# Two feed-forward down projections of a decoder layer, from plain row blocks to seven block products

## The chip, the cores and the metric

One core of one Trainium2 chip runs the whole program. The metric is device time in microseconds (us) of that core. Three runs of the kernel before took 2435.83 to 2436.16 us, median 2435.97. One more execution was profiled; all rows below are from it.

## What is computed

A decoder layer over 1024 tokens with a model width of 1024, in float32. The stages in order are: a feed-forward half step, two token mixers (attention) that are merged by gates, a second feed-forward half step, and a gated embedding. The change is in the two feed-forward half steps:

```python
D_MODEL, SEQ, D_FF = 1024, 1024, 2816

def swiglu(u, w_in, w_out):
    a, b = jnp.split(u @ w_in, 2, axis=-1)
    return (jax.nn.silu(a) * b) @ w_out

h = h + 0.5 * swiglu(rms_norm(h, ffn1_norm), ffn1_w_in, ffn1_w_out)
...
h = h + 0.5 * swiglu(rms_norm(h, ffn2_norm), ffn2_w_in, ffn2_w_out)
```

`u @ w_in` is the up projection, `hidden @ w_out` the down projection. The hidden matrix is 1024 tokens by 2816 features, 22 feature blocks of 128.

## The kernel before, in words

**Arithmetic.** Every float32 operand is split into a rounded part HI (fp32r) and a remainder LO, and each product is three matmuls: HI by HI, HI by LO, LO by HI (`mm3`, L181 and on; L179 records each matmul). A split is one cast on ScalarE (ACT) and one subtraction on GpSimd (POOL): L138 and L139 in `load_split`.

**Up projection** (class `Up`, matmuls on L397). The up projection is already done by seven block products (Strassen-Winograd) in place of eight. The two halves of the weights' columns, a and b, and the two halves of the tokens give 2x2 blocks. For each feature block f, seven products of 12 matmuls run in the order 1, 6, 5, 2, 7, 3, 4 (the last f: 1, 6, 2, 5, 7, 3, 4). Products 6 and 7 add up in one bank of PSUM: product 6's bank is read by VectorE (DVE) on L420 into the tile `u2`, and only then may product 7 add to it. After product 4 a chain runs on DVE and ACT (L437, L438, L439, L440), and the finished hidden block, 128 features by 1024 tokens, is stored to DRAM (`hid_d`, one transfer of 512 KB, L441). The pool `upb` holds one buffer each of `u2`, `u3`, `p5` and `c21`, and two of `hidf`, the hidden block.

**Down projection** (class `Down`). Feature blocks go in groups of two (the last group has four). For each group, each of 8 token tiles t and each of two column halves c, one PSUM bank adds up 2 x 3 matmuls (128 by 128 weights, 512 columns) and DVE adds the bank to h at once (L253). While a group computes, the next one's hidden blocks and weight rows are loaded in transfers of 512 KB and split by ACT and POOL. In the last group, each finished token tile goes through `norm_tile`: square and sum on ACT (L216), two small operations on POOL (L197, L198), scaling on DVE (L218), and then, 9.5 us later in the order of TensorE (PE), eight transposes of `un` (L183) into two banks, each evicted by ACT (L207) and DVE (L208). `un` has three buffers. h is loaded from DRAM in eight transfers of 512 KB as soon as the up projection's buffers come free (L587, L1177).

**Order of the work.** PE's order is the order of the code, with the deferred transposes put in by a running count of PE's time (`tick`, `defer`). The instructions of the other engines and of the transfer queue (SP) are ordered ahead of time by a list scheduler, by code order among those that are ready in its own timeline; each engine then runs them strictly in that order. PSUM has eight banks, the pool `dpool` six buffers of split operands, `rawp` three buffers of raw loads, and `upool` four large ones.

```python
for f in self.groups[n]:
    ...
    out.append((load_split([(0, self.hid_d[f].unsqueeze(1))], 1024, homes[0]),
                w_rows(self.wo, f * P, 0, 1024, home=homes[1])))
```

Of the kernel before, what the change touches and what calls it, by code (L numbers as in the profile page):

```python
# [19 lines left out]
P = 128  # L20
S = 1024
# [26 lines left out]
def hybrid_layer_kernel(  # L48
# [242 lines left out]


    A_OF = {1: "a11", 2: "a12", 3: "s4", 4: "a22", 5: "s1", 6: "s2", 7: "s3"}

# [6 lines left out]
    class Left:  # L301
# [40 lines left out]
    class Up:  # L342


        def __init__(self, wi, hid_d):
            self.wi, self.hid_d, self.pools, self.ra, self.w = wi, hid_d, {}, {}, {}

# [36 lines left out]
        def block(self, f, left):  # L384
# [83 lines left out]
    class Down:  # L468


        def __init__(self, hid_d, wo):
            self.hid_d, self.wo, self.more, self.n = hid_d, wo, None, 0
            self.groups = [(f, f + 1) for f in range(0, NF - 4, 2)] + [tuple(range(NF - 4, NF))]

        def home(self):

            pool = dpool if self.n % 10 < 6 else self.more
            self.n += 1
            return pool.tile([P, 2, 1024], F32R, tag="D", name="D")

        def load(self, n):
            out = []
            for f in self.groups[n]:
                if n == len(self.groups) - 2:
                    both = upool.tile([P, 2, 2, 1024], F32R, tag="u", name="D2")
                    homes = both[:, 0], both[:, 1]
                else:
                    homes = self.home(), self.home()
                out.append((load_split([(0, self.hid_d[f].unsqueeze(1))], 1024, homes[0]),
                            w_rows(self.wo, f * P, 0, 1024, home=homes[1])))  # L490
            return out

        def run(self, ready, scale, h, prepare, after):
            for n in range(len(self.groups)):
                cur, last = ready, n + 1 == len(self.groups)
                if last:
                    prepare()
                else:
                    ready = self.load(n + 1)
                for t in down_chunk(h, [c[0] for c in cur], [c[1] for c in cur], scale):  # L500
                    if last:
                        after(t)


    hid_d = dram.tile([NF, P, S], F32, name="hid_d")
    st_u = ExitStack()
    ux = phase(st_u, "ux1", 3, "right")
    st_f = ExitStack()
    up = Up(ffn1_w_in, hid_d)
    up.open(st_f, "1", ("wb", "upa"))  # L510
# [64 lines left out]
    up.open(st_f, "1", ("upb",))  # L575
    down = Down(hid_d, ffn1_w_out)
    ready = []
    up.run(left1, ["s2", "a22", "s3", "s4"], lambda: ready.extend(down.load(0)))
    st_f.close()
    st_u.close()  # L580
    st_h = ExitStack()
    hp = phase(st_h, "h", 1, "right")
    st = ExitStack()
    down.more = phase(st, "dmore1", 4)
    h = hp.tile([P, NT, DM], F32, name="h")
    for t in range(NT):
        nc.sync.dma_start(out=h[:, t, :], in_=x[t * P:(t + 1) * P, :])  # L587
    gm = bcast_row(hp, mix_norm, DM)
    um = []

    def after1(t):
        norm_tile(hp, um, h, t, gm)
        nc.sync.dma_start(out=h_spill[t * P:(t + 1) * P, :], in_=h[:, t, :])

    down.run(ready, 0.5, h, lambda: um.extend(new_u()), after1)
    st.close()
    u = um
# [83 lines left out]
    st.close()  # L681
    st_h.close()
    st = ExitStack()
# [447 lines left out]

    up = Up(ffn2_w_in, hid_d)
    left2 = []
# [31 lines left out]
    up.open(st_f, "2", ("wb", "upa", "upb"))  # L1165
    down = Down(hid_d, ffn2_w_out)
    ready = []
    up.run(left2[0], ["a12", "s1", "s2", "s3", "s4", "a22"], lambda: ready.extend(down.load(0)))
    st_f.close()
    st_u.close()  # L1170
    st_h = ExitStack()
    hp = phase(st_h, "h3", 1, "right")
    st = ExitStack()
    down.more = phase(st, "dmore2", 4)
    h = hp.tile([P, NT, DM], F32, name="h3")
    for t in range(NT):
        nc.sync.dma_start(out=h[:, t, :], in_=h_spill[t * P:(t + 1) * P, :])  # L1177
    gp = bcast_row(hp, ple_norm, DM)
    u3 = []
    down.run(ready, 0.5, h, lambda: u3.extend(new_u()), lambda t: norm_tile(hp, u3, h, t, gp))  # L1180
    st.close()

# [27 lines left out]
    st.close()  # L1210
    st_h.close()
    st_p.close()
# [28 lines left out]
```

## Time and profile before

| what | value |
|---|---|
| median of three runs | 2435.97 us |
| the profiled execution, its own time | 2436.7 us |
| its span, first to last instruction | 2434.9 us |
| PE busy | 2355.5 us (97%) |
| DVE / ACT / POOL busy | 57% / 36% / 41% |
| up projections, about | 58 to 495 us, 1672 to 2096 us |
| down projections, about | 495 to 740 us, 2096 to 2341 us |

The profiled execution's own time lies 0.7 us over the median, and its span 1.8 us under its own time. Matmul durations overlap one another in the profile, so what one matmul costs is read from how many start in a stretch, not from its duration.

### The profile page before, as it was taken

The page shows a single profiled execution, that of the slowest core. Times are in us where ns is not written, and L with a number is a line of the kernel's source. Part 1 is how long each engine was busy: PE and PEld are TensorE (multiplying, and loading weights), DVE is VectorE, ACT ScalarE, POOL GpSimd, SP SyncE. Part 2 cuts the span into 40 slices and gives each one's busy share as a digit, 9 for nine tenths or more (in the row PEclk, how much of TensorE's full clock was granted, in tenths as well). Part 3 has the DMA queues.
Part 4 walks back from the last instruction along what each step waited for, and adds up shares of the span by engine and source line. Part 5 has one row for each costly group of instructions (what it writes and reads, how often), then busy time and mean ns, then how long its engine had stood idle before and what let it go on. Part 6 is the DMA issues. An engine that isn't in the chain of part 4 may idle for free.

```text
span 2434.9 us, 29649 instructions
## 1 busy us (share of the span) xinstructions
PE 2355.5 (97%) x11408; PEld 1965.2 (81%) x11408; DVE 1397.2 (57%) x1814; ACT 869.0 (36%) x1434; POOL 1002.0 (41%) x656
## 2 busy tenths in 40 slices
PE   6899999999999999989998998999999999999999
PEld 5788888888888898777777887887888888888887
DVE  5756666455552224657777778557566655455442
ACT  4433232321223233545656666225223323212131
POOL 7444444453523133432123432556444444545220
PEclk8999999999999999999999999999999999999999
DMA  6222222252425424794453566512222222523222
GB/s 218 76 78 78 79 94 88 87 200 88 136 87 141 108 76 120 213 228 101 99 111 89 143 176 193 182 70 78 87 78 84 90 87 78 216 87 121 69 87 78
DMA packets 246718, 279.91 MB, mean 115 GB/s; under 512 B 11696, under 2 KB 195248, under 8 KB 246576
## 3 DMA queue, kind: packets, MB, share of 16 engines
q1 hardware_dynamic: 222640, 244.46, 31.2%
q0 software_dynamic: 23936, 33.56, 6.7%
q8 instruction: 89, 1.46, 0.2%
q14 instruction: 53, 0.43, 0.1%
HBM read 196.19 MB, written 81.79 MB: 114 GB/s over the span
## 4 chain that ended last, share of the span: by engine, by line
PE 55%; DVE 6%; DMA 3%; ACT 2%; issue 2%; POOL 2%; SPq 0%; ACTq 0%; DVEq 0%; POOLq 0%
PE T L179 31%; PE T L397 17%; PE A L179 4%; PE T L183 3%; DVE D L990 1%; DVE D L991 1%; DMA raw<-in_w_in_dram 1%; DMA k_d<-ev 1%; POOL D L139 1%; DVE pt L208 1%; DVE D L1014 0%; POOL hid L258 0%; DVE mx L1010 0%; ACT D L987 0%; ACT D L1012 0%
## 5 line engine op out<-in xcount | busy, mean ns | idle before, releaser
L397 PE MATMUL T<-u,D 128*128 128x512 f32 x3168 | 734.2, 391 | 4.9 <-DVE u L420 2.6
L397 PEld LDWEIGHTS T<-u,D 128*128 128x128 f32 x3168 | 596.3, 189 | 130.8 <-DVE u L420 2.4
L139 POOL TENSOR_TENSOR D<-raw,D 128x1024 fp32r<-128x1024 f32 (+3 forms) x162 | 370.0, 2304 | 470.0 <-ACT D L138 443.8
L179 PE MATMUL T<-D 128*128 128x512 f32 x2208 | 509.3, 391 | 9.9 <-ACT D L207 5.9
L179 PEld LDWEIGHTS T<-D 128*128 128x128 f32 x2208 | 414.4, 189 | 96.8 <-ACT D L207 6.3
L253 DVE SCALAR_TENSOR_TENSOR h<-T,h 128x512 f32<-128x512 f32 x320 | 220.9, 691 | 226.6 <-PE T L179 224.5
L359 POOL TENSOR_TENSOR D<-ts,D 128x1024 fp32r<-128x1024 f32 x88 | 216.6, 2462 | 314.4 <-ACT D L358 314.3
L138 ACT CAST D<-raw 128x1024 fp32r<-128x1024 f32 (+3 forms) x162 | 157.6, 994 | 384.7 <-PE T L179 206.4
L179 PE MATMUL T<-u,D 128*128 128x512 f32 x1152 | 288.6, 398 | 3.4 <-DVE op L940 2.9
L179 PEld LDWEIGHTS T<-u,D 128*128 128x128 f32 x1152 | 213.3, 191 | 45.2 <-DVE op L940 4.4
L358 ACT CAST D<-ts 128x1024 fp32r<-128x1024 f32 x88 | 92.4, 1051 | 286.7 <-PE T L397 272.8
L179 PE MATMUL T<-D,u 128*128 128x512 f32 (+2 forms) x960 | 194.2, 361 | 0.0
L179 PEld LDWEIGHTS T<-D,u 128*128 128x128 f32 x960 | 166.6, 188 | 22.2
L374 DVE TENSOR_TENSOR ts<-raw 128x512 f32<-128x512 f32 x44 | 35.0, 795 | 202.0 <-POOL D L359 200.4
L208 DVE TENSOR_TENSOR pt<-T,pt 128x512 fp32r<-128x512 f32 (+1 forms) x160 | 100.9, 634 | 70.4 <-ACT pt L207 68.8
L359 POOL TENSOR_TENSOR D<-raw,D 128x1024 fp32r<-128x1024 f32 x44 | 120.4, 2737 | 34.1 <-ACT D L358 34.1
L179 PE MATMUL T<-pt,hv 128*128 128x256 f32 (+1 forms) x640 | 114.0, 301 | 13.9 <-DVE pt L208 12.7
L397 PE MATMUL T<-u,wb 128*128 128x512 f32 x528 | 126.8, 389 | 0.0
L179 PE MATMUL A<-hd 128*128 128x512 f32 (+5 forms) x480 | 114.9, 370 | 2.3 <-DMA hd<-sbk_d 1.6
L440 DVE TENSOR_TENSOR hidf<-u,sg 128x512 f32<-128x512 f32 x44 | 111.5, 2533 | 9.8 <-ACT sg L438 9.4
L207 ACT CAST pt<-T 128x512 fp32r<-128x512 f32 (+1 forms) x160 | 86.7, 544 | 83.8 <-PE T L183 82.1
L397 PEld LDWEIGHTS T<-u,wb 128*128 128x128 f32 x528 | 99.1, 188 | 20.6
(190 smaller groups left out, 2807.2 us busy)
## 6 DMA issues: line engine op xcount, KB each, us to landing
raw<-in_ffn_w_in_dram SPq DMA_DIRECT2D x88, 512.0 KB, 4.0
hid_d<-hidf SPq DMA_DIRECT2D x44, 512.0 KB, 2.6
raw<-hid_d SPq DMA_DIRECT2D x44, 512.0 KB, 3.2
raw<-in_ffn_w_out_dram SPq DMA_DIRECT2D x44, 512.0 KB, 3.5
raw<-in_w_in_dram SPq DMA_DIRECT2D x28, 512.0 KB, 4.4
h_spill<-h SPq DMA_DIRECT2D x16, 512.0 KB, 2.6
gate_d<-gate SPq DMA_DIRECT2D x16, 512.0 KB, 3.2
hd<-sbk_d POOLq DMA_DIRECT2D x32, 256.0 KB, 5.1
```

Source lines behind the costliest of these rows:

```text
L138: nc.scalar.copy(d[:, HI, :n], raw[:, :n])
L139: nc.gpsimd.tensor_sub(d[:, LO, :n], raw[:, :n], d[:, HI, :n].bitcast(F32))
L179: nc.tensor.matmul(ps, lhs, rhs, start=start, stop=stop)
L183: nc.tensor.transpose(ps, src, ident)
L207: nc.scalar.copy(hi, ps)
L208: nc.vector.tensor_sub(lo, ps, hi.bitcast(F32))
L253: nc.vector.scalar_tensor_tensor(hs, ps, scale, hs, op0=ALU.mult, op1=ALU.add)
L358: nc.scalar.copy(d[:, HI], src)
L359: nc.gpsimd.tensor_sub(d[:, LO], src, d[:, HI].bitcast(F32))
L374: nc.vector.tensor_sub(ts[:, 0], b12, b11)
L397: nc.tensor.matmul(ps, b[:, l, k], a[:, r, k], start=start and k == n == 0, stop=k == 3 and n == 2, skip_group_check=True)
L440: nc.vector.tensor_mul(t["hid"][:, 512:], u3, sg)
```

## The change

Both down projections are done by the same seven block products as the up projection. The blocks are: token halves by the two feature blocks of a pair on the left, the two feature blocks by column halves on the right. There are 11 pairs of feature blocks. Seven left operands per pair (a11, a12, a22 and the sums s1 to s4) are formed on DVE at the end of the up projection's odd blocks and stored as seven 256 KB pieces. The down projection runs over 77 steps; a step is one product of one pair, 12 matmuls into four banks. Products 1 and 2 alternate pair by pair, then 5, 7, 6, 3 and 4 run over all pairs, one after another. A product's four banks add up over all 11 pairs before they are evicted. The subtraction of a split moves from POOL to DVE, except for the first two pairs. The sums on the right are kept in `upool`. h is loaded within step 10's code, and token tiles are normalised four at a time, after products 3 and 4.

```diff
     def new_u():
-        return [[upool.tile([P, KT, 512], F32R, tag="u", name="u") for _ in range(2)] for _ in range(2)]
+        return [upool.tile([P, KT, 512], F32R, tag="u", name="u") for _ in range(2)]
...
+    HS = {name: n for n, name in enumerate(("a11", "a12", "a22", "s1", "s2", "s3", "s4"))}
...
                 nc.vector.tensor_mul(t["hid"][:, 512:], u3, sg)
-                nc.sync.dma_start(out=self.hid_d[f], in_=t["hid"])
+                store("a12" if f % 2 else "a11", c12_of(t["hid"]))
+                if f % 2 == 0:
+                    self.even = t["hid"]
+                    return
+                a11, a21, a12, a22 = (x[:, c:c + 512] for x in (self.even, t["hid"]) for c in (0, 512))
+                store("a22", a22)
+                s1, s4 = tmp("upb", "c21"), tmp("upb", "u2")
+                nc.vector.tensor_add(s1, a21, a22)
+                nc.vector.tensor_sub(a21, a11, a21)
+                nc.vector.tensor_sub(a11, s1, a11)
+                nc.vector.tensor_sub(s4, a12, a11)
+                for name, src in (("s1", s1), ("s3", a21), ("s2", a11), ("s4", s4)):
+                    store(name, src)
+            def store(name, src):
+                nc.sync.dma_start(out=self.hs_d[f // 2, HS[name]], in_=src)
...
+            self.steps = [(k, i) for i in range(self.N) for k in (1, 2)]
+            self.steps += [(k, i) for k in (5, 7, 6, 3, 4) for i in range(self.N)]
...
+        def right(self, raw, c0, k, r, c, n=1):
+            src = self.wo[r * P:(r + n) * P, c * 512:(c + 1) * 512]
+            nc.sync.dma_start(out=raw[:, c0:c0 + n * 512].rearrange("q (k c) -> q k c", k=n),
+                              in_=src.rearrange("(k q) c -> q k c", q=P))
+        def left(self, raw, name, i):
+            nc.sync.dma_start(out=raw[:, :512], in_=self.hs_d[i, HS[name]])
+        def sums(self, kind, i):
+            key, n = (kind, i) if i < 8 else ("rest", i - 8 + 3 * (kind == 3))
+            if key not in self.tt:
+                self.tt[key] = upool.tile([P, 8, 512], F32, tag="u", name="tt")
+            return self.tt[key][:, n]
+        def step_tile(self):
+            self.done += 1
+            pool = self.more if self.more is not None and self.done % 7 == 0 else dpool
+            return pool.tile([P, 2, 1024], F32R, tag="D", name="D")
+        def split(self, d, src, cols, eng):
+            nc.scalar.copy(d[:, HI, cols], src)
+            eng.tensor_sub(d[:, LO, cols], src, d[:, HI, cols].bitcast(F32))
+        def load(self, k, i, eng):
+            if k == 2:
+                return
+            whole, a, b = slice(0, 1024), slice(0, 512), slice(512, 1024)
+            if k == 1:
+                ra, rb, rc = self.new_raw(False), self.new_raw(False), self.new_raw()
+                self.left(ra, "a11", i)
+                self.right(ra, 512, k, 2 * i, 0)
+                self.left(rb, "a12", i)
+                self.right(rb, 512, k, 2 * i + 1, 0)
+                self.right(rc, 0, k, 2 * i, 1, 2)
+                for kk, r in ((1, ra), (2, rb)):
+                    self.d[kk, i] = self.step_tile()
+                    self.split(self.d[kk, i], r, whole, eng)
+                nc.vector.tensor_sub(self.sums(1, i), rc[:, a], ra[:, b])
+                nc.vector.tensor_sub(self.sums(3, i), rc[:, b], rc[:, a])
+                return
+            raw = self.new_raw()
+            d = self.d[k, i] = self.step_tile()
+            self.left(raw, A_OF[k], i)
+            if k == 3:
+                self.right(raw, 512, k, 2 * i + 1, 1)
+                self.split(d, raw, whole, eng)
+                return
+            t = self.sums(1 if k == 5 else 3, i)
+            if k in (7, 6):
+                self.right(raw, 512, k, 2 * i + (k == 6), 0)
+            self.split(d, raw[:, a], a, eng)
+            self.split(d, t, b, eng)
+            if k == 7:
+                nc.vector.tensor_add(t, t, raw[:, b])
+            elif k == 6:
+                nc.vector.tensor_sub(t, t, raw[:, b])
...
+        def run(self, scale, open_raws, open_norm, h_of, after):
+            def acc(out, x, f):
+                nc.vector.scalar_tensor_tensor(out, x, f, out, op0=ALU.mult, op1=ALU.add)
...
+            def evict(k, j, ps, x, h):
+                h11, h12, h21, h22 = (h[:, j + 4 * r, c * 512:c * 512 + 512] for r in range(2) for c in range(2))
+                if k == 1:
+                    nc.scalar.copy(x["p1"][:, j], ps)
+                    acc(h11, ps, scale)
+                elif k == 2:
+                    acc(h11, ps, scale)
+                elif k == 5:
+                    nc.scalar.copy(x["p5"][:, j], ps)
+                elif k == 7:
+                    nc.vector.tensor_add(x["w"][:, j], ps, x["p1"][:, j])
+                elif k == 6:
+                    nc.vector.tensor_add(x["p1"][:, j], ps, x["p1"][:, j])
+                    nc.vector.tensor_add(x["w"][:, j], ps, x["w"][:, j])
+                    u2, u3, p5 = x["p1"][:, j], x["w"][:, j], x["p5"][:, j]
+                    for out, v in ((h12, u2), (h12, p5), (h21, u3), (h22, u3), (h22, p5)):
+                        acc(out, v, scale)
+                elif k == 3:
+                    acc(h12, ps, scale)
+                    after(j)
                 else:
...
+                    acc(h21, ps, -scale)
+                    after(4 + j)
+            ahead, x, h = 5, {}, None
+            loaded = 4
...
+            for n, (k, i) in enumerate(self.steps):
+                while loaded < len(self.steps) and loaded <= n + ahead:
+                    self.load(*self.steps[loaded], nc.vector)
+                    loaded += 1
+                if n == 10:
+                    h = h_of()
+                if i == 0:
+                    pss[k] = [bank() for _ in range(4)]
+                d = self.d.pop((k, i))
+                for j in range(4):
+                    tok = slice(j * P, (j + 1) * P)
+                    mm3(pss[k][j], d[:, HI, tok], d[:, LO, tok], d[:, HI, 512:], d[:, LO, 512:],
+                        i == 0, i == self.N - 1)
+                if i == self.N - 1:
+                    for j, ps in enumerate(pss.pop(k)):
+                        evict(k, j, ps, x, h)
...
+    def early():
+        for i in range(2):
+            down.load(1, i, nc.gpsimd)
...
+    def run_down(down, name, h_src, gain, spill):
...
+        def open_raws(d):
+            d.raws = phase(st_r, "raws" + name, 4, "right")
+            d.more = phase(st, "dmore" + name, 1)
+            d.temps = phase(st, "temps" + name)
+        def h_of():
+            h = box["h"] = hp.tile([P, NT, DM], F32, name="h")
+            for t in range(NT):
+                nc.sync.dma_start(out=h[:, t, :], in_=h_src[t * P:(t + 1) * P, :])
+            return h
...
+        def after(t):
+            if t % 4 == 0:
+                u.append(new_u())
+            norm_tile(box["n"], u, box["h"], t, box["g"])
```

In `new_raw(False)` the buffer comes from the four of `raws` once that pool is open, and else from `rawp`. The new pools lie where the up projection's lay.

## Rows read from the trace of the kernel before

**Rows 1.** The page: the span, and each engine's busy time
```profile
span 2434.9 us, 29649 instructions
PE 2355.5 (97%) x11408; PEld 1965.2 (81%) x11408; DVE 1397.2 (57%) x1814; ACT 869.0 (36%) x1434; POOL 1002.0 (41%) x656
```

**Rows 2.** The chain of waits in order of time: start, length, what
```profile
1706.75 389.30 PE T L397 x1716
2096.04 211.26 PE T L179 x932
```

**Rows 3.** The timeline of PE in down projection 1: start, length, instructions, idle before
```profile
495.07 211.42 PE L179 MATMUL T<-D 128*128 128x512 f32 x932
706.33 1.03 PE L183 MATMUL T<-ident,un 128*128 128x128 f32 x8
750.37 1.06 PE L183 MATMUL T<-ident,un 128*128 128x128 f32 x8 [0.23 <-DVE un L218]
```

**Rows 4.** Groups by shape: busy us, mean ns of one | idle before, releasers
```profile
L139 POOL TENSOR_TENSOR D<-raw,D 128x1024 fp32r<-128x1024 f32 x136 | 328.4, 2438 | 377.3 <-ACT D L138 351.2 <-DVE D L990 18.5 <-issue 6.0
L253 DVE SCALAR_TENSOR_TENSOR h<-T,h 128x512 f32<-128x512 f32 x320 | 220.9, 691 | 226.6 <-PE T L179 224.5 <-DMA h<-in_x_dram 1.0
L138 ACT CAST D<-raw 128x1024 fp32r<-128x1024 f32 x136 | 139.5, 1050 | 367.1 <-PE T L179 189.2 <-DMA raw<-in_ffn_w_out_dram 70.2 <-PE T L397 34.2
L218 DVE SCALAR_TENSOR_TENSOR un<-h,r,gbc 128x1024 f32<-128x1024 f32 x16 | 20.4, 1277 | 1.3 <-POOL r L198 1.2
```

**Rows 5.** The timeline around the end of one feature block, up projection 1
```profile
259.51 0.69 DVE L374 TENSOR_TENSOR ts<-raw 128x512 f32<-128x512 f32 x1 [5.56 <-POOL D L359]
260.12 0.69 DVE L376 TENSOR_TENSOR ts<-raw 128x512 f32<-128x512 f32 x1
...
263.87 16.48 PE L397 MATMUL T<-u,D 128*128 128x512 f32 x72
...
266.79 0.69 DVE L437 TENSOR_TENSOR c<-u,T 128x512 f32<-128x512 f32 x1 [0.18 <-PE T L397]
...
267.97 2.49 POOL L359 TENSOR_TENSOR D<-ts,D 128x1024 fp32r<-128x1024 f32 x1 [1.90 <-ACT D L358]
268.45 2.56 DVE L440 TENSOR_TENSOR hidf<-u,sg 128x512 f32<-128x512 f32 x1 [0.24 <-ACT sg L438]
...
272.30 0.69 DVE L420 TENSOR_TENSOR u<-T,p 128x512 f32<-128x512 f32 x1 [1.29 <-PE T L397]
...
276.13 2.39 POOL L359 TENSOR_TENSOR D<-ts,D 128x1024 fp32r<-128x1024 f32 x1 [5.67 <-ACT D L358]
```

**Rows 6.** Transfers by line: count, KB each, median us from issue to landing
```profile
hid_d<-hidf SPq DMA_DIRECT2D x44, 512.0 KB, 2.6
pp_d<-po SPq DMA_DIRECT2D x16, 256.0 KB, 2.3
```

**Rows 7.** Windows: us, busy of PE, PEld, DVE, ACT, POOL, clock, DMA share, GB/s
```profile
500.00:502.00 2.00, 2.00 (x10) 1.65 (x10) 1.40 (x3) 0.00 (x0) 1.83 (x1) 1.00 1.03 422
520.00:700.00 180.00, 180.00 (x796) 149.04 (x795) 89.68 (x131) 36.00 (x37) 84.53 (x38) 1.00 0.34 110
```

**Rows 8.** The timeline of the transfer queue: the loads of h
```profile
492.54 4.44 SPq L587 DMA_DIRECT2D h<-in_x_dram  x8
2085.19 3.95 SPq L1177 DMA_DIRECT2D h<-h_spill  x8
```

**Rows 9.** Timelines of ACT, POOL, DVE: one token tile's norm
```profile
702.72 1.06 ACT L216 ACTIVATE un<-h 128x1024 f32<-128x1024 f32 x1 [4.29 <-DVE h L253]
703.68 0.18 ACT L216 ACTIVATION_READ_ACCUMULATOR un<-h 128x1 f32 x1
...
704.22 0.55 POOL L198 TENSOR_TENSOR r<-r,mhalf 128x1 f32<-128x1 f32 x1
705.32 1.28 DVE L218 SCALAR_TENSOR_TENSOR un<-h,r,gbc 128x1024 f32<-128x1024 f32 x1
...
707.58 1.29 DVE L208 TENSOR_TENSOR u<-T,u 128x512 fp32r<-128x512 f32 x2 [0.99 <-ACT u L207]
```

More of the change, by code (lines that the diff above doesn't have):

```diff
@@ L468, in hybrid_layer_kernel @@
     class Down:
[L471 to L478, printed above, removed]
-            return pool.tile([P, 2, 1024], F32R, tag="D", name="D")
[L481 to L486, printed above, removed]
-                else:
[L488 to L505, printed above, removed]
+        N = NF // 2
@@ new lines, in left, with new_raw @@
+        def left(self, raw, name, i):
[5 more added lines that the diff above has]
+            return self.tt[key][:, n]
+        def new_raw(self, early=True):
+            pool = rawp if early or self.raws is None else self.raws
+            return pool.tile([P, 1024], F32, tag="raw", name="raw")
@@ L506, in hybrid_layer_kernel @@
+    hs_d = dram.tile([NF // 2, 7, P, 512], F32, name="hs_d")
     st_u = ExitStack()
@@ L575, in hybrid_layer_kernel, with open_norm @@
     up.open(st_f, "1", ("upb",))
-    down = Down(hid_d, ffn1_w_out)
-    ready = []
-    up.run(left1, ["s2", "a22", "s3", "s4"], lambda: ready.extend(down.load(0)))
+    down = Down(hs_d, ffn1_w_out)
+    def early():
+        for i in range(2):
+            down.load(1, i, nc.gpsimd)
+    up.run(left1, ["s2", "a22", "s3", "s4"], early)
     st_f.close()
     st_u.close()
[L581 to L596, printed above, removed]
+    def run_down(down, name, h_src, gain, spill):
+        st_h, st_n, st_r, st = (ExitStack() for _ in range(4))
+        hp = phase(st_h, "h" + name, 1, "right")
+        u, box = [], {}
+        def open_raws(d):
[7 more added lines that the diff above has]
+            return h
+        def open_norm():
+            st_r.close()
+            box["n"] = phase(st_n, "norm" + name, 1, "right")
+            box["g"] = bcast_row(box["n"], gain, DM)
+        def after(t):
+            if t % 4 == 0:
+                u.append(new_u())
+            norm_tile(box["n"], u, box["h"], t, box["g"])
+            if spill:
+                nc.sync.dma_start(out=h_spill[t * P:(t + 1) * P, :], in_=box["h"][:, t, :])
+        down.run(0.5, open_raws, open_norm, h_of, after)
+        st.close()
+        return box["h"], u, (st_n, st_h)
+    h, um, st_h = run_down(down, "1", x, mix_norm, True)
     u = um
@@ L681, in hybrid_layer_kernel @@
     st.close()
-    st_h.close()
+    for s_ in st_h:
+        s_.close()
     st = ExitStack()
@@ L1165, in hybrid_layer_kernel, with early2 @@
     up.open(st_f, "2", ("wb", "upa", "upb"))
-    down = Down(hid_d, ffn2_w_out)
-    ready = []
-    up.run(left2[0], ["a12", "s1", "s2", "s3", "s4", "a22"], lambda: ready.extend(down.load(0)))
+    down = Down(hs_d, ffn2_w_out)
+    def early2():
+        for i in range(2):
+            down.load(1, i, nc.gpsimd)
+    up.run(left2[0], ["a12", "s1", "s2", "s3", "s4", "a22"], early2)
     st_f.close()
     st_u.close()
[L1171 to L1181, printed above, removed]
+    h, u3, st_h = run_down(down, "2", h_spill, ple_norm, False)
     st = ExitStack()
@@ L1210, in hybrid_layer_kernel @@
     st.close()
-    st_h.close()
+    for s_ in st_h:
+        s_.close()
     st_p.close()
```

22 lines of the change are left out of this document (18 added, 4 removed).

## The prediction

> **What bounds the kernel now.** I read the page first: PE is busy for 97% of the span, DVE for 57%, ACT and POOL less [rows 1]. Such a share is an average, so the chain of waits comes next: it runs through PE without a break for 389.3 us of the second up projection and for 211.3 us of the second down projection [rows 2]. The timeline of PE says the same of down projection 1: 932 matmuls in 211.42 us, with only 0.23 us of waiting at its end [rows 3]. So both feed-forward stages are bound by the number of PE's instructions, at 211.26/932 = 0.2267 us a matmul in a down and 389.30/1716 = 0.2269 in an up projection, which is already done by block products. Whatever the change puts on other engines is free as long as it stays beside PE.
>
> **What it removes.** A down projection has 22 blocks x 8 token tiles x 2 halves x 3 = 1056 matmuls; after, 77 steps x 12 = 924. That is 2 x 132 = 264 fewer, at 0.2267 us: **-59.9 us**. The transposes stay as many. A step takes 12 x 0.2267 = 2.72 us, the 77 of them 209.5 us.
>
> **Does the work on the other engines fit?** Per down projection DVE loses 160 evictions of 0.691 us, 111 us [rows 4]. It gains 29 whole subtractions (18 in steps 1 and 2, 11 in step kind 3; the four early ones stay on POOL), nearest row the 1.277 us of L218 with its two wide inputs [rows 4]; 88 half subtractions and 44 right sums, and 48 eviction operations, all 512 wide, which follow each other at 0.61 us (259.51 to 260.12) [rows 5]: 37 + 80.5 + 29.3 = 147 us of 209.5. ACT has 33 casts of 1.05 us [rows 4], 88 of half the width and 8 copies, 129 operations of at most that, under 136 us; POOL is nearly empty. On average all is hidden, so their cost is put at nothing, covered by PE's 2.72 us a step; five places remain where an average does not tell.
>
> **1. The joint of two blocks in the up projection: 0.3 us each, 6 us in all.** The sum s4 takes the only buffer `u2`. The next block's product 6 can be read out (L420) only when s4's store has landed, and product 7 waits for that read. In the rows, 72 matmuls (products 4, 1, 6, 5, 2, 7) run from 263.87, so product 7 starts at 263.87 + 5 x 2.72 = 277.47. The hidden block is finished at 268.45 + 2.56 = 271.01. Four sums at 0.61 us end at about 273.5 [rows 5]. A 256 KB store lands 2.3 us after issue, one of 512 KB 2.6 [rows 6]; with five stores in a row I take 2.9: 276.4, and then L420's 0.69 us makes 277.1. That leaves 0.4 us, so nothing or a fraction is lost: 0 to 1.2 us (the upper end has the store land 1.5 us later), 0.3 taken because the slack is that thin. There are 10 such joints in each of two up projections: bounds 0 and 24 us. The store on SP is queued behind the four others, which are ready earlier, and ahead of nothing due soon.
>
> **2. The start of the down projection: 5 + 3 us.** Products 1 and 2 need six 256 KB pieces a pair, 1.573 MB in two steps (5.44 us), and h is 4.19 MB more. Nine pairs (two are early) and h make 18.3 MB in the 54.4 us of the first 20 steps: 337 GB/s. The row with h's load shows 422 GB/s at a share of 1.03, 410 at full use; the steady down projection shows 110 at 0.34, 324 at full use [rows 7]. So the stage needs 45 to 57 us of transfer in 54, and order matters. h's code stands at step 10, but in the rows its loads start as soon as buffers come free, 2.5 us ahead of the first down projection (492.54 against 495.07) and 10.9 us ahead of the second (2085.19 against 2096.04) [rows 2, 3, 8], and the scheduler can do that again. Then pairs 2 and 3 go first (there are raw buffers for two pairs), h next, pair 4 behind it: 492.5 + 2.3 + 2 x 3.84 + 10.2 + 3.84 = 516.5, plus cast and subtraction 2.3, is 518.8, against a need at 495.07 + 8 x 2.72 = 516.8: 2 us late; by 324 GB/s in place of 410 it is 8 us. Both rows are equally near (one has large rows in one queue, the other the same mixture of loads), so I take the middle, 5. In the second, h is done as the step count starts but meets the early pair 1: 3 us. Bounds for the two: 0 and 16.
>
> **3. The eviction of product 6: 1 us each, 2 in all.** It puts 28 operations of 0.61 us, 17.1 us, on DVE within 2 us of the end of step 54. Split operands for steps 55 to 60 are ready by then (seven buffers), 16.3 us of PE. Step 61's subtraction queues behind: done at -2 + 17.1 + 1.3 = 16.4. If step 60's is caught too, PE waits 2.8. Bounds 0 and 6 for both.
>
> **4. The norm in fours: 2.5 + 2 us, 9 in all.** Before, token tiles finish one after another, and no transpose waits more than 0.23 us [rows 3]. Now four finish together and all their transposes stand at one place of PE's order, but `un` has three buffers: the fourth tile's square can start only when the first tile's transposes (8 in 1.03 us [rows 3]) are done. Its chain is 1.06 + 0.18 on ACT, about 0.8 on POOL and 1.28 on DVE, 702.72 to 706.60 in the rows [rows 9]: some 3.7 us. PE has two more tiles' transposes, 1.7 us, to do in that time: 2 us lost. For the first four, half of PSUM is held by product 4, and the transposes wait for L208 (1.29 us a tile [rows 9]) as well: 2.5. Bounds over the four places: 2 and 16.
>
> **5. Edits at nothing.** The seven stores put 0.79 MB more a pair beside 38 us of the up projection; the next phase's weights are loaded while the last steps run, and if that cover went, one load and split (about 3 + 1.05 + 2.44 us) would show. The edges of products find their four banks free: product 1's are read during step 21.
>
> **Sum.** 59.9 - 6 - 8 - 2 - 9 = 34.9 us. From the profiled execution's 2436.7 us this gives 2401.8; the median is 0.7 lower, so **2401 us**. All bounds at their low end cost 2 us (2378), all at their high end 62 (2438).
>
> **Where the skill speaks against the change.** Rows: L440, with both inputs in SBUF, took 2.56 us where such an operation otherwise takes 0.69, and it ended just after POOL's subtraction of 267.97 to 270.46 had [rows 5]. The Trainium skill, SBUF — State Buffer, "Who interferes with whom", says that a DVE instruction with two SBUF inputs and a GpSimd instruction that reads SBUF exclude each other for the whole instruction. By that rule, the trace agrees, the four new sums of a joint can each be held up; the result is rival B. In the rows POOL stands still from 270.46 to 276.13, just where the sums fall, which is why I keep 0.3 us [rows 5].
>
> The same skill, DMA: Bandwidth & Descriptors, "Bandwidth", asks for transfers of 1 MiB or more and has 138 GB/s at 64 KB, 341 at 1 MB; 240 for 256 KB would be an estimate between them, the first 20 steps would take 76 us in place of 54, and the sum would come to about 2437. Nothing here shows so low a rate with several transfers under way.
>
> **Rivals.**
> A, nearly all is hidden: the scheduler keeps h's load out of the way, the stores land in time, the norm's chains overlap. For it: PE has hardly waited in these stages [rows 3]. Against: the three buffers of `un`. Costs of 2 to 12 us: 2378 to 2388, say 2384.
> B, **slower**, one mechanism: the joint. If a POOL subtraction moves into the sums' window, s4 comes 2.4 us later [rows 4], product 7 then 2.4 + 0.3 us late at 20 joints: 54 us in place of 6, so 2450. It decides from (59.9 - 19)/20 = 2.0 us a joint. Against it stands the idle of POOL there.
> C, the start of the down projection is bound by transfers: at 324 GB/s, and h ahead of everything (13 us), pair 4 comes some 13 us late in both: 26 in place of 8, 2419.
> D, the saving does not show: with matmuls of the same shape at 0.2267 us in both projections I see no way but the sum of several mishaps; 2436.
>
> **How the numbers follow.** Forecast (costs of 12 to 40 us: 2388 to 2416) 0.62; A 0.13; C 0.14; B 0.06; D 0.05. The likeliest gives 2401. The range takes in A and C with the bounds of the parts: 2382 to 2428, leaving out B, D and the tails, some 0.17. A measurement tells 0.2% (4.9 us) from no change: faster 0.90, same 0.04, slower 0.06.
>
> **What would show it.** 924 matmuls of L179's kind in each down projection at 0.227 us, and a stage of some 209.5 + 6.9 us of transposes and waits. Part 1 is right if PE waits at L397 for L420 by under half a microsecond ten times in each up projection; wrong, towards B, at 2 us. Part 2 shows as a wait of PE within steps 4 to 20 for a split of DVE that itself waited for a transfer, with h's eight loads ahead of it on the queue; part 3 as a wait near step 61; part 4 as four waits of 2 us at L183 for `un`, 10 us after products 3 and 4. The prediction is wrong if the stage of products 1 and 2 lasts over 75 us, or the up projection grows by over 25.

## The result

The changed kernel takes 2400.79 us (median of 4 runs, 2397.77 to 2401.92), the kernel before 2436.06 in the same comparison: a ratio of 0.9853, 95% interval 0.9836 to 0.9870. That is 35.3 us less, where 35 were forecast. The profiled execution was the lowest of the four, 2397.77 us with a span of 2396.0; its span is 38.9 us under the one of before. One run of the kernel with the left sums alone, 2950.15 us at a mean granted clock of 0.749, is left out of its median below. The page of after, against [rows 1]:

```profile
span 2396.0 us, 29982 instructions
PE 2304.2 (96%) x11144; PEld 1920.5 (80%) x11144; DVE 1529.9 (64%) x2000; ACT 956.9 (40%) x1604; POOL 821.0 (34%) x576
```

PE has 11144 instructions for 11408, 264 fewer as counted. POOL gave 181 us of work away, and DVE has 133 more. The timeline of PE in after, from the start of down projection 1 to the end of the first projections of the next stage (start, length, instructions, idle before and its releaser), shows what came of the saving, against [rows 3]; behind the dots follow the waits of PE and the places of the transposes in down projection 2:

```profile
494.75 32.80 PE L179 MATMUL T<-D 128*128 128x512 f32 x144
528.40 0.50 PE L179 MATMUL T<-D 128*128 128x512 f32 x1 [0.84 <-ACT D L527]
529.66 156.97 PE L179 MATMUL T<-D 128*128 128x512 f32 x691 [0.76 <-DVE D L528]
686.47 1.91 PE L183 MATMUL T<-ident,un 128*128 128x128 f32 x16
688.61 0.66 PE L183 MATMUL T<-ident,un 128*128 128x128 f32 x4 [0.23 <-DVE u L208]
689.99 0.66 PE L183 MATMUL T<-ident,un 128*128 128x128 f32 x4 [0.73 <-DVE u L208]
691.78 1.25 PE L183 MATMUL T<-ident,un 128*128 128x128 f32 x8 [1.14 <-DVE u L208]
692.79 20.25 PE L179 MATMUL T<-D 128*128 128x512 f32 x88
712.87 10.14 PE L179 MATMUL T<-u,D 128*128 128x512 f32 x44
722.85 1.47 PE L183 MATMUL T<-ident,un 128*128 128x128 f32 x12
...
728.17 2.82 PE L183 MATMUL T<-ident,un 128*128 128x128 f32 x12 [1.14 <-DVE u L208]
730.64 79.05 PE L179 MATMUL T<-u,D 128*128 128x512 f32 x340
809.53 11.46 PE L179 MATMUL T<-D,u 128*128 128x384 f32 x65
...
2112.66 156.93 PE L179 MATMUL T<-D 128*128 128x512 f32 x691 [0.47 <-DVE D L528]
2269.43 1.91 PE L183 MATMUL T<-ident,un 128*128 128x128 f32 x16
...
2275.76 20.25 PE L179 MATMUL T<-D 128*128 128x512 f32 x88
...
2305.82 2.66 PE L183 MATMUL T<-ident,un 128*128 128x128 f32 x20
...
2312.73 78.22 PE L179 MATMUL T<-D,u 128*128 128x512 f32 x340
```

144 + 1 + 691 + 88 = 924 matmuls stand where 1056 stood, at 156.97/691 = 0.2272 us. PE is late twice at the start, 0.84 and 0.76 us, and then without a gap until the transposes. Those take 692.79 - 686.47 = 6.32 us for the first four token tiles and 730.64 - 722.85 = 7.79 for the others; one tile's eight transposes took 0.79 us before (706.33 to 707.12), so four need 3.2. By stages, from the same points of both timelines:

| stretch | before | after | difference |
|---|---|---|---|
| to the start of down projection 1 | 495.07 | 494.75 | -0.3 |
| down projection 1, to the next stage's first matmul | 244.72 | 218.12 | -26.6 |
| the next stage's first 384 matmuls | 89.29 | 96.66 | +7.4 |
| from there to the start of down projection 2 | 1266.80 | 1269.63 | +2.8 |
| down projection 2, as above | 244.72 | 216.68 | -28.0 |
| the rest | 94.30 | 100.16 | +5.9 |
| span | 2434.9 | 2396.0 | -38.9 |

The rows of a down projection flatter the change a little. Before, six token tiles were transposed within it and two behind it; after, there are four and four, so 1.6 us of transposes (2 x 0.79) moved from one row to the next. Tile for tile the down projections give 25.0 and 26.4 us of 29.9 each, and 5.8 and 4.3 us are given back behind them, where the transposes of the second four tiles stand. The 2.8 us in between are 1.2 in the rest of the token mixers, whose code did not change (831.84 us before, 833.03 after, up to the first matmul of the second up projection), and 1.6 in that up projection (434.96 and 436.60). The mixers take 830.8 to 838.8 us in the profiles of this case, so their part is scatter.

### The profile page after: what moved, and what is told of

It is laid out like the page before. It is cut to its first block, busy times and chain, and to the rows that moved or that the text cites. A ratio compares the mean times of both kernels' runs of the same rounds, so it can differ in the third digit from the quotient of the medians.

```text
span 2396.0 us, 29982 instructions
## 1 busy us (share of the span) xinstructions
PE 2304.2 (96%) x11144; PEld 1920.5 (80%) x11144; DVE 1529.9 (64%) x2000; ACT 956.9 (40%) x1604; POOL 821.0 (34%) x576
## 4 chain that ended last, share of the span: by engine, by line
PE 77%; DVE 7%; DMA 6%; issue 4%; POOL 3%; ACT 2%; SPq 0%; ACTq 0%; DVEq 0%; POOLq 0%
PE T L179 36%; PE T L401 34%; PE A L179 4%; PE T L183 3%; DMA raw<-in_ffn_w_out_dram 2%; DVE D L1131 1%; POOL D L139 1%; DMA k_d<-ev 1%; DVE D L1132 1%; DMA raw<-in_w_in_dram 1%; DVE D L1155 1%; DVE pt L208 1%; POOL hid L259 0%; DVE u L208 0%; POOL D L363 0%
## 5 line engine op out<-in xcount | busy, mean ns | idle before, releaser
L401 PE MATMUL T<-u,D 128*128 128x512 f32 x3168 | 734.2, 391 | 6.2 <-DVE u L424 3.8
L401 PEld LDWEIGHTS T<-u,D 128*128 128x128 f32 x3168 | 596.0, 189 | 132.3 <-DVE u L424 4.1
L179 PE MATMUL T<-D 128*128 128x512 f32 x1944 | 449.0, 392 | 12.0 <-ACT D L207 5.8
L179 PEld LDWEIGHTS T<-D 128*128 128x128 f32 x1944 | 366.2, 189 | 90.6 <-ACT D L207 6.3
L139 POOL TENSOR_TENSOR D<-raw,D 128x1024 fp32r<-128x1024 f32 (+4 forms) x74 | 159.9, 2168 | 287.8 <-ACT D L138 281.4
L527 ACT CAST D<-raw 128x512 fp32r<-128x512 f32 (+1 forms) x154 | 123.5, 807 | 225.7 <-PE T L179 113.2
L197 POOL TENSOR_SCALAR r<-ss 128x1 f32<-128x1 f32 (+1 forms) x56 | 19.3, 345 | 485.7 <-ACT un L217 404.5
L528 DVE TENSOR_TENSOR D<-raw,D 128x512 fp32r<-128x512 f32 (+1 forms) x146 | 131.0, 900 | 62.3 <-ACT D L527 61.1
L208 DVE TENSOR_TENSOR pt<-T,pt 128x512 fp32r<-128x512 f32 (+1 forms) x160 | 100.9, 634 | 69.4 <-ACT pt L207 67.8
L401 PE MATMUL T<-u,wb 128*128 128x512 f32 x528 | 126.8, 389 | 0.0
L207 ACT CAST pt<-T 128x512 fp32r<-128x512 f32 (+1 forms) x160 | 86.8, 545 | 83.8 <-PE T L183 82.2
L401 PEld LDWEIGHTS T<-u,wb 128*128 128x128 f32 x528 | 99.1, 188 | 20.6
```

The lines of the kernel that those rows point to most:

```text
L139: nc.gpsimd.tensor_sub(d[:, LO, :n], raw[:, :n], d[:, HI, :n].bitcast(F32))
L179: nc.tensor.matmul(ps, lhs, rhs, start=start, stop=stop)
L207: nc.scalar.copy(hi, ps)
L208: nc.vector.tensor_sub(lo, ps, hi.bitcast(F32))
L401: nc.tensor.matmul(ps, b[:, l, k], a[:, r, k], start=start and k == n == 0, stop=k == 3 and n == 2, skip_group_check=True)
L527: nc.scalar.copy(d[:, HI, cols], src)
```

## Experiments

Each kernel was compared with the kernel before on the same chip; differences from the changed kernel are between medians, and "the kernel beside it" is the changed kernel as run again, at 2399.64 us, unless another is named. Three chips were used, on which the medians of the kernel before were 2435.84 to 2437.35 us, so such a difference can be off by 1 or 2 us. Executions of one kernel scatter by 2 to 12 us here, so a gain of a few microseconds is read from the trace as well.

**The same kernel again.**

> The changed kernel once more, unchanged, as the measure for the runs beside it and for a second profile. Theory: 264 matmuls fewer at 0.2267 us (-59.9 us), and given back in four places: the norm of token tiles in fours (about 14 us of transposes and waits more than the transposes alone), the start of each down projection (2 us), one joint of the up projection (1.3 us), the rest 1 to 4 us. So about 2400 us again, 34 to 38 below the kernel before. Rival: its runs differed by 4 us where those of before differ by 1, so a part of the time hangs on the transfers' chance order; then the second profile shows another wait at the start of a down projection than the 2.1 us of the first (up to 6).

2399.64 us (2395.02 to 2406.79), ratio 0.9855 (0.9838 to 0.9872). The profiled execution was the longest, 2406.79 us. The same waits of PE stand in it at the start of down projection 1, 0.6 us longer, and none at the start of the second; but the granted clock differs. The timeline of PE, and a window of 4 us (us, busy time of PE, PEld, DVE, ACT, POOL, granted clock, DMA share, GB/s):

```profile
529.95 0.50 PE L179 MATMUL T<-D 128*128 128x512 f32 x1 [1.45 <-ACT D L527]
531.21 158.54 PE L179 MATMUL T<-D 128*128 128x512 f32 x691 [0.76 <-DVE D L528]
```
```profile
532.00:536.00 4.00, 4.00 (x13) 3.13 (x12) 3.78 (x5) 2.10 (x2) 0.00 (x0) 0.61 1.05 405
```

After the two waits PE was granted a mean of 0.61 of its clock in the next 4 us, that is 1.2 GHz for the larger part of them, and the 691 matmuls took 158.54 us in place of 156.97. In the first profile, with waits of 1.60 us in place of 2.21, the clock stayed at 1.00 there. So the scatter is in part the clock's, but not for the most part: of the 9.0 us between the spans of the two profiles, 3.8 lie in down projection 1 and 5.8 in the mixers (838.81 us against 833.03), whose code is the same in all kernels; why the mixers scatter is open. The rival's wait of up to 6 us did not come.

**The transposes spread over the next stage's matmuls.**

```diff
-            norm_tile(box["n"], u, box["h"], t, box["g"])
+            norm_tile(box["n"], u, box["h"], t, box["g"], 9500.0 + 2722.0 * (t % 4))
```

> The transposes of the four token tiles of a half are deferred by 9.5, 12.2, 14.9 and 17.7 us in place of 9.5 each; nothing else is changed. Theory (the norm in fours costs PE the time in which the transposes' banks wait for the evictions): the four places shrink from 6.3, 7.8, 6.3 and 6.9 us to about 3.2 us each, so 12 to 15 us faster than the changed kernel, near 2387. Rival (the eviction is the bound wherever the transposes stand, or the delayed ones stall the next stage): no gain, 2400 or more.

2383.97 us (2380.93 to 2386.63), ratio 0.9787 (0.9774 to 0.9800): 15.7 us under the kernel beside it, a little over the theory's 12 to 15. The timeline of PE at the second place of down projection 1:

```profile
722.17 1.03 PE L183 MATMUL T<-ident,un 128*128 128x128 f32 x8
722.96 2.30 PE L179 MATMUL T<-u,D 128*128 128x512 f32 x9
725.10 1.25 PE L183 MATMUL T<-ident,un 128*128 128x128 f32 x8
```

Eight transposes again take 0.8 to 1.0 us, with no wait. What cost the changed kernel time there was not the work but its place in PE's order: the four bundles stood at one point.

**A fourth buffer of `un`.** This tests the cause that the prediction gave for its part 4.

```diff
...
-            norm_tile(box["n"], u, box["h"], t, box["g"])
+            un = None
+            if t == 3:
+                un = down.temps.tile([P, 4, 512], F32, tag="p5", name="un", bufs=1)
+                un = un.rearrange("q a b -> q (a b)")[:, :1024]
+            norm_tile(box["n"], u, box["h"], t, box["g"], un=un)
```

> The fourth token tile of the first half gets a buffer of its own for the normalised tile (in the tile p5, free by then), so its square need not wait for the first tile's transposes. Theory of the prediction (the three buffers of un are what PE waits for): the first half's place loses its 2 to 2.5 us in both down projections, 4 to 5 us in all, and PE no longer waits there. Rival (the four free banks, each evicted by ACT and DVE, are what it waits for): waits of 0.2 and 0.7 us for the evictions stay, and only the fourth tile's own ACT and DVE operations leave the middle of the burst: 1 to 2.5 us in all.

2396.48 us (2393.52 to 2398.83), ratio 0.9839 (0.9826 to 0.9851); 3.2 us under the kernel beside it, with ranges that overlap, so by the time alone unclear. The timeline of PE decides:

```profile
687.62 1.91 PE L183 MATMUL T<-ident,un 128*128 128x128 f32 x16
691.49 2.45 PE L183 MATMUL T<-ident,un 128*128 128x128 f32 x16 [1.96 <-DVE u L208]
693.69 20.21 PE L179 MATMUL T<-D 128*128 128x512 f32 x88
```

The place lasts 6.07 us, as against 6.32; in the second down projection it lasts 6.69, as against 6.33. PE still does 16 transposes into the four banks that product 4 does not hold, and then waits for L208, the eviction of a bank, now once for 1.96 us in place of three times for 2.10 in all. So one buffer more of `un` does not free PE: what ends its wait is a bank. But the run does not tell what the buffer alone is worth, because the list scheduler also ordered DVE anew: five splits now run there before the first eviction, which starts 3.1 us after the transposes (690.75 against 687.62) in place of 1.4. The last of the splits, and the evictions:

```profile
690.15 0.68 DVE L528 TENSOR_TENSOR D<-raw,D 128x512 fp32r<-128x512 f32 x1
690.75 4.86 DVE L208 TENSOR_TENSOR u<-T,u 128x512 fp32r<-128x512 f32 x8
```

**Without h's loads.**

```diff
-                nc.sync.dma_start(out=h[:, t, :], in_=h_src[t * P:(t + 1) * P, :])
+                nc.gpsimd.memset(h[:, t, :], 0.0)
```

> Leaves out the eight loads of h in both down projections (h is set to zero by GpSimd in their place), so the residual is missing from the result. Theory (PE waits in the first twenty steps only because h's 4.19 MB stand among the pairs' transfers): PE's waits at the start, 1.6 and 0.5 us in the first profile and more in the other runs, go to nothing, and the runs lie closer together: 2 to 6 us faster than the changed kernel. Rival (the pairs' own 1.57 MB each are what it waits for, or the waits have another cause): the same waits stay, 0 to 1 us.

2394.62 us (2390.33 to 2401.81), ratio 0.9825 (0.9811 to 0.9839): 5.0 us under the kernel beside it, with ranges that overlap, so by the time alone unclear. PE runs from the first step to the transposes without a wait, in the second down projection too:

```profile
497.22 189.66 PE L179 MATMUL T<-D 128*128 128x512 f32 x836
```

So h's transfers are what made PE late. The runs did not lie closer together (11 us), so that part of the expectation fell; the waits of the norm, and the clock after them, were still there.

**The price of a joint, both ways.** First s4 in another buffer, then the four sums on the slower engine.

```diff
-                s1, s4 = tmp("upb", "c21"), tmp("upb", "u2")
+                s1, s4 = tmp("upb", "c21"), tmp("upb", "u3")
```

> The sum s4 is formed in the buffer u3, which the next block needs only after its product 7, in place of u2. Theory (the joint of two blocks costs little: 0.3 us by the prediction's working, one wait of 1.3 us and no other in the profile): 1 to 3 us faster than the changed kernel. Rival (the joints cost more than the rows show, 1 us each): 20 us faster.

2399.35 us (2396.07 to 2404.63), ratio 0.9845 (0.9830 to 0.9861): 0.3 to 1.4 us under the two sets of runs of the changed kernel, no more than the scatter; that excludes the rival's 20 us. The trace shows the gain: PE's waits for L424 are back at what those for L420 were in the kernel before (us, times; first after, then this kernel), and the second up projection takes 434.99 us, as in the kernel before (434.96), in place of 436.60.

```profile
  PE T L401: 3.8, 4
```
```profile
  PE T L401: 2.6, 3
```

```diff
-                nc.vector.tensor_add(s1, a21, a22)
-                nc.vector.tensor_sub(a21, a11, a21)
-                nc.vector.tensor_sub(a11, s1, a11)
-                nc.vector.tensor_sub(s4, a12, a11)
+                nc.gpsimd.tensor_add(s1, a21, a22)
+                nc.gpsimd.tensor_sub(a21, a11, a21)
+                nc.gpsimd.tensor_sub(a11, s1, a11)
+                nc.gpsimd.tensor_sub(s4, a12, a11)
```

> The four sums of a joint are formed on GpSimd in place of VectorE. An operation of that shape took 1.34 us there against 0.72 between starts on VectorE, so s4 is ready about 2.5 us later. Theory (product 7 of the next block waits for u2, which waits for s4's store, with 0.4 to 0.7 us of slack): PE waits about 2 us at each of 20 joints, 35 to 50 us slower than the changed kernel, 2435 to 2450. Rival (the store's landing is not what product 7 waits for): no change, within 3 us.

2441.10 us (2436.47 to 2444.06), ratio 1.0012 (1.0004 to 1.0021): 40 to 41 us slower than the changed kernel, and a little slower than the kernel before. One joint in its timeline, and what ended DVE's idle time ahead of L424 over the whole run (us, times):

```profile
324.29 1.29 POOL L455 TENSOR_TENSOR u<-hidf 128x512 f32<-128x512 f32 x1
...
325.61 0.32 SPq L460 DMA_DIRECT2D hs_d<-u  x1
...
327.69 0.69 DVE L424 TENSOR_TENSOR u<-T,p 128x512 f32<-128x512 f32 x1 [7.58 <-DMA hs_d<-u]
...
328.44 1.88 PE L401 MATMUL T<-u,D 128*128 128x512 f32 x7 [1.71 <-DVE u L424]
```
```profile
  DMA hs_d<-u: 151.9, 20
```

s4 is done at 325.58, its store lands 2.08 us after its issue, L424 takes 0.69, and product 7 starts 1.71 us late: the chain of the prediction's part 1, in each of 20 joints. PE's waits for L424 grew from 3.8 to 37.0 us. So a late s4 costs what the prediction's rival B said in kind; that a POOL subtraction would delay the sums on DVE, which was B's reason for it, is not what this run makes.

**The matmuls alone.**

```diff
-                    mm3(pss[k][j], ..., i == 0, i == self.N - 1)
+                    for rep in range(2 if k == 4 else 1):
+                        mm3(pss[k][j], ..., i == 0 and rep == 0,
+                            i == self.N - 1 and (k != 4 or rep == 1))
```

> Every matmul of product 4 in both down projections is issued twice, so the lower left quarter is scaled wrongly; 264 matmuls more, as many as the change removes, with no more loads, splits or evictions. Theory (the down projections are bound by PE's instructions): 59.9 us slower than the changed kernel, about 2460, which is 24 us above the kernel before: what the change gives back. Rival (the down projection is now bound by transfers or VectorE, and the saving of matmuls is only partly got): clearly less than 60, 20 to 45.

2461.89 us (2456.73 to 2463.45), ratio 1.0094 (1.0080 to 1.0109): 61.1 us over the changed kernel for 264 matmuls, 0.231 us each (62.3 over the changed kernel as run again; 59.8 when each of the two is taken against the kernel before that ran beside it). The rival's 20 to 45 did not come: the down projections are still bound by the count of PE's instructions.

**The left sums alone, in the kernel before.**

```diff
...
                 nc.sync.dma_start(out=self.hid_d[f], in_=t["hid"])
+                if f % 2 == 0:
+                    self.even = t["hid"]
+                    return
...
+                s1, s4 = tmp("upb", "c21"), tmp("upb", "u2")
+                nc.vector.tensor_add(s1, a21, a22)
...
+                for m, src in enumerate((s1, a21, a11, s4)):
+                    nc.sync.dma_start(out=hs_d[f // 2, m], in_=src)
```

> The kernel before with the four sums of each pair formed in the up projections and stored (11 x 4 stores of 256 KB more each), and nothing else of the change; the down projections read the plain blocks as before. Theory (the sums and stores lie beside PE, with a thin slack at 20 joints): 0 to 6 us slower than the kernel before. Rival (the left sums are a cost of their own that the saved matmuls pay for): 10 us or more slower.

2440.82 us against 2435.95, ratio 1.0021 (1.0012 to 1.0030): 4.9 us slower, within the theory's 0 to 6. PE's waits for L421, which is L420 here, are only 3.0 us in its profile, where the kernel before had 2.6. The span of that profile is 3.0 us over the one of before: 0.3 by the start of down projection 1, 0.9 in the second up projection, and 1.6 in the mixers, which scatter by more than that. So the joints are a small part of it; where the rest of the 5 us lies is not settled.

**Two and three edits together.** The first takes spread and s4 in `u3`; the second, on top, issues h's loads behind the last pair's.

> Both edits together: the transposes of the four token tiles spread over 8.2 us more, and s4 in the buffer u3. Theory: the gains add up, 13 to 18 us faster than the changed kernel, near 2385. Rival: one of them has no gain of its own, or the waits move to the next place; then no better than the better of the two alone.

> spread_s4 once more, beside h_after_pairs: theory and rival both expect about 2382 us; its profile shows whether the wait in the first twenty steps (3.1 us in its first profile) comes back.

> On top of spread_s4 the eight loads of h are issued behind the transfers of the last pair, so nothing is left out, only their place in the queue changes. Theory (PE waits in the first twenty steps because h's transfers stand between the pairs'): no wait of PE between the first step and step 20, no fall of the granted clock there, 3 to 5 us faster than spread_s4. Rival (the stage moves as many bytes either way, 93% of it at full transfer rate, and the wait only moves to h's first use after step 20): no gain.

```diff
...
-            for t in range(NT):
-                nc.sync.dma_start(out=h[:, t, :], in_=h_src[t * P:(t + 1) * P, :])
+            with tc.issue_after(down.last.ins):
+                for t in range(NT):
+                    nc.sync.dma_start(out=h[:, t, :], in_=h_src[t * P:(t + 1) * P, :])
...
-                if n == 10:
+                if n == 15:
```

Here `down.last` is the last weight load that was issued. spread_s4 took 2381.94 us (ratio 0.9768, 0.9754 to 0.9782) and again 2383.18 (0.9784, 0.9771 to 0.9797), 16 to 18 us under the kernel beside it. That is 1 to 2 us better than spread, within the scatter; its second up projection, at 434.97 and 435.01 us, shows the gain of `u3` once more. PE waited 3.13 and 1.74 us at the start of down projection 1 in its two profiles. With h behind the pairs it is 2377.27 us (2375.43 to 2378.88), ratio 0.9759 (0.9746 to 0.9771): 5.9 us under spread_s4 beside it, with ranges that do not overlap; the theory had 3 to 5. Its timelines of PE and of the transfer queue, and the window of the first steps:

```profile
495.91 189.66 PE L179 MATMUL T<-D 128*128 128x512 f32 x836
```
```profile
524.51 1.41 SPq L718 DMA_DIRECT2D h<-in_x_dram  x3
```
```profile
494.00:530.00 36.00, 36.00 (x161) 29.80 (x160) 30.72 (x37) 15.14 (x15) 0.00 (x0) 1.00 1.02 373
```

The transfers are as busy as ever (share 1.02), but PE is busy for all 36 us at full clock: the order of the same bytes was what cost time. The second down projection has no wait either. Of the 6.9 us between the spans of the two profiles 3.9 lie in down projection 1 and the 384 matmuls behind it (307.82 and 303.89 us); 2.9 are the mixers' scatter. This is the fastest version, 58.7 us under the kernel before, close to the 59.9 that the matmuls alone promise.

## Why the prediction was right, and where not

**The saving.** -59.9 us for 264 matmuls: right. Doubling as many cost 61.1, and where nothing waits 836 of them take 189.66 us, 0.2269 each.

**Part 1, the joint: 6 forecast, 1.2 measured.** The chain is as described (sums_on_pool shows it), the size was off. PE's waits at L401 for L424 are 3.8 us where those for L420 were 2.6, and the difference is one joint of the twenty. The term that was mis-sized is the landing of s4's store: it mostly took less than the 2.9 us that I used, as the summary of all stores of line L460 in after has it:

```profile
DMA to landing us min/median/max: 2.0/2.0/9.7
```

The timeline of after has a usual joint, and the one that was late, near the end of the second up projection:

```profile
313.82 0.69 DVE L424 TENSOR_TENSOR u<-T,p 128x512 f32<-128x512 f32 x1 [2.14 <-ACT D L362]
...
317.95 2.88 PE L401 MATMUL T<-u,wb 128*128 128x512 f32 x12
...
2046.83 1.73 SPq L460 DMA_DIRECT2D hs_d<-u  x1
...
2051.05 0.69 DVE L424 TENSOR_TENSOR u<-T,p 128x512 f32<-128x512 f32 x1 [4.24 <-DMA hs_d<-u]
...
2051.79 3.06 PE L401 MATMUL T<-u,D 128*128 128x512 f32 x12 [1.27 <-DVE u L424]
```

On the first, L424 ends at 314.51 and product 7 starts at 317.95 - 2.72 = 315.23, 0.7 us of slack; on the second the store took 4.2 us. Its issue alone took 1.73 us, where it takes 0.32 on a usual joint. The down projection's early loads, the new traffic there, were not in its way: the last of them was issued at 2039.96 and landed 4.0 us later, before this store was issued. What held the store up is open.

**Part 2, the start: 8 forecast, 2.1 in the profile (0.84 + 0.76 and 0.47), 5 by the runs without h.** In all nine profiles of kernels that leave h in its place the waits are 1.6 to 3.1 us in the first down projection and 0 to 0.5 in the second. The cause is right, as no_h_load and h_after_pairs show. The transfer queue of after, a cast that waited, and the window of the first 60 us:

```profile
498.29 0.91 SPq L504 DMA_DIRECT2D raw<-in_ffn_w_out_dram  x2
499.25 0.97 SPq L717 DMA_DIRECT2D h<-in_x_dram  x2
```
```profile
527.30 1.05 ACT L527 CAST D<-raw 128x1024 fp32r<-128x1024 f32 x1 [6.56 <-DMA raw<-in_ffn_w_out_dram]
```
```profile
494.75:554.80 60.05, 58.45 (x257) 47.83 (x256) 45.15 (x57) 26.87 (x34) 0.00 (x0) 1.00 0.93 346
```

The scheduler put h's eight loads between the pairs' one or two at a time, not in a block ahead of pair 4 as I reckoned, so their 10 us were shared out over several pairs, and the wait came at step 12 (after 144 matmuls) and not at step 8. The transfers reached 403 to 416 GB/s between 508 and 520 us, the upper of my two rates, in pieces of 256 and 512 KB. The rule of the Trainium skill, DMA: Bandwidth & Descriptors, "Bandwidth", to move 1 MiB or more at a time, by which the sum would have been 2437, does not bind here: that rate was reached by pieces of a quarter and half of that size, several of them under way.

**Part 3, the eviction of product 6: 2 forecast, nothing measured.** The step that failed is that step 61's subtraction "queues behind" the 28 operations. DVE is busy for 29.23 of the 30 us from 645 to 675, but the list scheduler put the splits (L528) among the evictions:

```profile
645.34 0.68 DVE L584 TENSOR_TENSOR w<-T,w 128x512 f32<-128x512 f32 x1
645.93 1.21 DVE L528 TENSOR_TENSOR D<-raw,D 128x1024 fp32r<-128x1024 f32 x1
```

**Part 4, the norm in fours: 9 forecast, 14.7 measured, and the wait that ends last was another.** The four places last 6.32, 7.79, 6.33 and 6.91 us, 27.4 in all against 12.7 for 16 tiles at 0.79. That the four tiles at one point cost this is shown by spread. The step that failed is that PE waits for the buffers of `un`; in the rows each of its waits ends with a bank. Thirty-two transposes fill eight banks; four are free at the first place (16 transposes go without a wait), three at the second of down projection 1 (12 go), and each is freed by a cast on ACT (L207) and a subtraction on DVE (L208), which also have the splits and the fourth tile's norm to do. I had named that as an addition of 0.5 us; it is the bound. The chain that I had reckoned runs close behind it. The fourth tile's scaling at the first place:

```profile
689.85 1.27 DVE L219 SCALAR_TENSOR_TENSOR un<-h,r,gbc 128x1024 f32<-128x1024 f32 x1
```

That tile is ready at 691.12, 0.66 us before PE goes on at 691.78. With banks enough PE would have finished three tiles at 686.47 + 3 x 0.79 = 688.84 and waited 2.3 us for it, an estimate from these rows and near the 2 us of the prediction. So the prediction's wait is hidden under a longer one; how the 14.7 us divide between the evictions, the fourth tile's norm and the splits in front of them, no run shows.

**What no part had: the clock.** The windows of after around the second place:

```profile
724.00:728.00 4.00, 1.64 (x11) 0.92 (x9) 3.06 (x4) 3.16 (x7) 0.74 (x2) 0.93 0.00 0
728.00:732.00 4.00, 3.83 (x15) 3.62 (x16) 3.04 (x6) 1.76 (x3) 0.00 (x0) 0.50 0.00 0
732.00:736.00 4.00, 4.00 (x14) 3.13 (x13) 1.03 (x2) 0.59 (x1) 0.00 (x0) 0.72 0.17 38
```

PE had run at 1.00 up to 724 us, was busy for 1.64 of 4 us between its waits, and then was granted 0.50, 1.2 GHz. The matmuls behind the transposes of the kernel before, first for down projection 1 and then for 2, are the measure:

```profile
751.19 78.05 PE L179 MATMUL T<-u,D 128*128 128x512 f32 x343
2351.58 78.00 PE L179 MATMUL T<-D,u 128*128 128x512 f32 x343
```

After, 340 of them took 79.05 and 78.22 us. At 0.227 us for each of the three fewer that is 1.7 and 0.9 us more, 2.6 in all; what the transposes themselves lost at the lower clock is within the 14.7. In spread, without the waits, the clock stayed at 1.00 from 690 to 740 us. The Trainium skill, TensorE: Matmul & The Clock Gate, "A second HAM failure mode: psum-queue depth-cycling", describes this: short idle times between groups of matmuls, from cycling through banks, let the clock swing. The rows agree with it in kind, with one fall and rise at the second place of each down projection and none at the first.

**The sum.** 59.9 - 1.2 - 2.1 - 0 - 14.7 - 2.6 = 39.3, and 38.9 are measured; the mixers' 1.2 us and some tenths elsewhere, more and less, make up the rest. That the total came out so close is luck: three terms that were too high (16 for 3.3) met one that was too low and one that was missing (9 for 17.3). The forecast was right by its saving and by the sign and order of its costs, not by the size of each. Rivals: A (costs of 2 to 12 us) fell to the place of the transposes, 21 us being given back in all. B's delay did not come: the four sums of a pair take 0.68 to 0.69 us each in all 22 pairs of after, so no POOL subtraction held them up, and no run made that happen; sums on POOL made the rest of its chain, at 1.7 us of PE a joint. C's mechanism is there but small. Its price of 13 us a projection does not follow from my own figures either: with h ahead of pairs 2, 3 and 4 at 324 GB/s, pair 4 is 8 us late as in part 2, and pair 2 is 492.5 + 2.3 + 12.9 + 4.9 + 2.3 - (495.07 + 4 x 2.72) = 9 us late.

## What to carry to other kernels

When work that came spread out comes in bundles, ask what each bundle fills and what empties it: here four tiles' transposes needed eight banks of which four were free, and moving them apart by 2.7 us each was worth 15.7 us, nearly half of what the whole change brought. A list scheduler pulls a load forward to where its buffer is free, not where its code stands; where transfers are the limit, tie it to the place where it may wait. A wait that is charged by count (20 joints) deserves an experiment that makes it longer: it gives the slack and the price at once.

## What was not expected of the hardware

Waits of 0.5 to 1.5 us on PE, a few in a row, were followed by windows of 4 us with a granted clock of 0.50 to 0.65. Whether it fell differed between executions of the same kernel, and the length of the wait did not decide it: at the start of down projection 1 the clock stayed at 1.00 after waits of 1.60 us (after) and 2.27 (un_four), and windows behind them had 0.61 after 2.21 us (again) and 0.75 to 0.82 after 2.42 (spread). And transfers of 256 and 512 KB, several under way, moved 401 to 416 GB/s between 508 and 536 us, nearly as much as the 422 of the larger loads before [rows 7].
